# Order of the decay exponentials, half of bk on GpSimd, the last gates' tiles, and T4 ahead of T1 in a fox-attention + RWKV-7 block

## The chip, the cores and the metric

One core of one Trainium2 chip. The metric is the device time of one execution in microseconds (us). Engines: PE = TensorE (matrix products), DVE = VectorE, ACT = ScalarE, POOL = GpSimd, SP = the queue that issues most of the DMAs. Each engine takes its instructions in the order in which they stand in its queue; one engine meets another only where an instruction waits for a semaphore.

## The reference

One residual block over 1024 tokens of width 1024, float32:

```python
u = modulate(rms_norm(h), shift1, scale1)
proj = u @ w_in                               # fox q,k,v,f | rwkv r,k,v,w,a,g | two gates
o_fox  = fox_attention(q, k, v, log_f)        # 8 heads of 64, causal, forget-gate bias
o_rwkv = rwkv7_time_mix(p_rwkv, ...)          # 8 heads of 64, state 64x64
merged = sigmoid(gate_fox) * (o_fox @ fox_w_out) + sigmoid(gate_rwkv) * (o_rwkv @ rwkv_w_out)
h = h + gate1 * (merged @ w_o)
u2 = modulate(rms_norm(h), shift2, scale2)
a, b = split(u2 @ w_up); a = causal_conv3(a) + conv_b
h = h + gate2 * ((silu(a) * b) @ w_down)
return rms_norm(h, final_g)
```

The RWKV-7 mix runs, for each token, `state = state * w + (state a) b^T + v k^T` and `y = state r`, with `w = exp(-exp(w_log))`; the kernel does it in chunks of 64 tokens, and the products of decays inside a chunk are exponentials of a running sum, exp(-DEC*cum) and exp(+DEC*cum).

## The kernel before

**Stages.** Normalisation and low-rank inputs (0 to about 120 us of the profiled span), the fox and RWKV projections and the first RWKV preparation (to 240), the RWKV units with projections and, from about 450, the output gates between their matmuls (240 to 615), attention by heads with the remaining gates between (615 to 830), the two branch products and `w_o` (to 1005), the up projection of the feed-forward part in 22 column blocks (1005 to 1430), and the down projection (to 1647). Large products are done in three passes: both operands are split into a high and a low part (`u_hi`, `u_lo`; `hi_in`, `lo_in`), and high x high, low x high and high x low are added in PSUM.

**Who sets the order.** PE's order is written out by a small planner, `Weave`, which runs generators of matmuls against each other by estimated times, so it is fixed when the program is made. In the RWKV stage the order of DVE, ACT, SP and POOL is set by the tile framework's scheduler, from the order of the code, data and buffer dependencies, and its own timing; the kernel can add a dependency between two instructions (`tc.add_manual_dep`), which the scheduler then keeps as an order. In attention and from the up projection on, the order on DVE and ACT (there on SP too) is that of the code.

**The RWKV units.** There are eight units, k = 0..7: four pairs of heads (p) by two halves of the sequence (hf) of 512 tokens, eight chunks of 64 each. Three things go on at once. The main chain of unit k: `sp` matmuls (L141) add the old state into the chunk's sum, ACT scales the result into the next state S (L903), one chunk after another (the second half of a pair needs seven states, the first eight); then `yp`, the copy `y` (L915) and the group norm. Two units ahead, `pre` makes the operands of unit k+2: `ar` (L737, L741), `bk` (L739, L744), of which a copy of one half is repeated (L740), then the pair products `p` and `E` (L764), a triangular solve in steps of DVE (`t`, L784, and `E`, L786) on masks `M` that come by `sm` (L772) and `M` (L776) over SP. Three units ahead, the decay: `cum` is loaded by SP (L711) from DRAM, scanned by DVE (L715), and `el`, `en` are made from it by ACT (L719, L721). `cum`, `el`, `en` and `bk` have one buffer each: a new `el` waits for the reader of the old one (`ar`, L741), a new `en` for the old one's (`bk`, L744), a new load of `cum` for the old one's (`en`, L721).

**The gates.** `gate_steps` makes one gate in two halves: a product `gt` in PSUM, then on ACT Abs (L337), Exp (L338), Ln (L339), on DVE a difference (L340), on ACT the last Exp (L341), and SP writes the result `gs` to DRAM (`d_gate`, L342). The tile `gs` comes from a pool (`gsp`, tag `sp0`). At the passage to attention the heads' operands (`stA`, `stB`, `vh`) are loaded by POOL's queue. The gates made during attention have one PSUM tile, `rk_ps`, which two ACT instructions (L1162, L1163) read before the next product may write it. The softmax of the first key blocks uses a tile with the tag `Ps` of the pool `at`, two buffers.

**The up projection.** A column block takes seven products, k = 1..7 (a 2x2 scheme of Strassen's kind), each of one sum of quarters of the weights and one sum of quarters of the input: k=4 uses the input sum T4 (tiles `T_h`), k=5 the sum T1 (tiles `T_m`, `T_e`), k=3 B22 (`B_e`, `B_m`). PE takes them in the order of `plan` (L1606, L1607), entries (block, k), and their operands are made some products ahead on ACT and DVE. Results (`X`, `Y`, `W`) are taken from PSUM by ACT copies (L1559, L1568).

Of the kernel before, what the change touches and what calls it, by code (L numbers as in the profile page):

```python
# [9 lines left out]
F32 = mybir.dt.float32  # L10
F32R = mybir.dt.float32r
AF = mybir.ActivationFunctionType
# [4 lines left out]
S = 1024  # L17
KT = 8
NH = 512
# [7 lines left out]
DEC = math.exp(-0.5)  # L27
# [8 lines left out]
NOSYNC = mybir.DependencyInfo(mybir.DependencyClass.NoSync, mybir.DependencyReason.DATA)  # L36
# [96 lines left out]
def hybrid_block(ctx: ExitStack, tc: tile.TileContext, a, out):  # L133
    nc = tc.nc
# [107 lines left out]
            nc.vector.tensor_tensor(dst[:, cs], ps, bb[:, cs], op=ALU.add)  # L242

    marks = {}
    late_lo = deque()

    def lower(wait=0):
# [79 lines left out]
    def gate_steps(w, i, pps, ptag, pool, tag):  # L327
        if weave.late == 1:
            yield from late_gate(w, i)
            return  # L330
        for hf in range(2):
            cs = slice(hf * NH, hf * NH + NH)
            ps = pps.tile([128, NH], F32, tag=ptag, name=f"gt{i}_{hf}")
            yield from gemm_steps(ps, w, u, cs)

            g = pool.tile([128, NH], F32, tag=tag, name=f"gs{i}_{hf}")
            nc.scalar.activation(g, ps, AF.Abs)  # L337
            nc.scalar.activation(g, g, AF.Exp, scale=-1.0)  # L338
            nc.scalar.activation(g, g, AF.Ln, bias=1.0)  # L339
            stt(g, ps, 0.0, g, op0=ALU.min, op1=ALU.subtract)  # L340
            nc.scalar.activation(g, g, AF.Exp)  # L341
            nc.sync.dma_start(d_gate[i, :, cs], g)  # L342


# [1 line left out]
    with ExitStack() as es:  # L346
# [7 lines left out]
        def gen(name):  # L354
            return pr.tile([128, NH], F32, tag="gen", name=name)
# [202 lines left out]
        with tc.tile_pool(name="lg", bufs=1, reuse_waits="tile") as lg, \  # L558
# [47 lines left out]
            last = []  # L606
# [68 lines left out]
        def c3(ap):  # L675
            return ap.rearrange("p (c s) -> p c s", s=CH)
# [21 lines left out]
        def pre(k, p, hf):  # L698
# [5 lines left out]
            def tmp(nm, w=NH, bufs=1, dt=F32):  # L704
                return rw.tile([128, w], dt, tag=nm, name=f"{nm}{n}", bufs=bufs)

            def chunk_tile(nm, bufs, *dims):
                return rw.tile([128, *dims], F32, tag=nm, name=f"{nm}{n}", bufs=bufs)

            cum = tmp("cum")  # L710
# [5 lines left out]
                                             op0=ALU.mult, op1=ALU.add)  # L716
            el = chunk_tile("el", 1, NCU, CH + 1)
            nc.gpsimd.memset(el[:, :, 0:1], 1.0)
            nc.scalar.activation(el[:, :, 1:], c3(cum), AF.Exp, scale=-DEC)  # L719
            en = tmp("en")  # L720
            nc.scalar.activation(en, cum, AF.Exp, scale=DEC)  # L721
            ksq = tmp("ksq")
            nc.scalar.activation(ksq, kk, AF.Square, scale=V("k_k", p))
            parts = rw.tile([128, 3, NH], F32R, tag="bk", name=f"kp{n}")
# [8 lines left out]
            bk = chunk_tile("bk", 1, NCU, 3, CH)  # L733
# [3 lines left out]
            stt(ar[:, 0], c3(kr), nkk[:, p : p + 1], el[:, :, 0:CH], op0=ALU.mult, op1=ALU.mult)  # L737
            stt(kr, kr, V("k_k", p), al, op0=ALU.mult, op1=ALU.mult)
            tt(bk[:, :, 0, :], c3(kr), c3(en), op=ALU.mult)  # L739
            nc.scalar.copy(bk[64:128, :, 2, :], bk[64:128, :, 0, :])  # L740
            tt(ar[:, 1], c3(rr), el[:, :, 1:], op=ALU.mult)  # L741
            ts(al, al, V("k_a", p), oka[:, p : p + 1], op0=ALU.mult, op1=ALU.add)
            tt(al, al, kk, op=ALU.mult)
# [1 line left out]
            pcd = chunk_tile("pcd", 3, NCU)  # L745
# [11 lines left out]
            for c0 in range(0, NCU, 4):  # L757
                ps = [gen(f"p1_{n}{h}{c0}") for h in range(2)]
# [42 lines left out]
            vt, at = gen(f"vt{n}"), gen(f"at{n}")  # L801
# [11 lines left out]
            ps = [gen(f"tb{n}{h}") for h in range(2)]  # L813
# [16 lines left out]
        def main(k, p, hf):  # L830
# [3 lines left out]
            pcd, ar, E, QA, TT, bon, UV = (o[k] for k in ("pcd", "ar", "E", "QA", "TT", "bon", "UV"))  # L834
# [6 lines left out]
            for h in range(2):  # L841
                i = nc.vector.transpose(X[B0[h], :, :], TT[B0[h], :, 0:32])
# [20 lines left out]
            for c0 in range(0, NCU, 4):  # L863
                ps = gen(f"uw{n}{c0}")
                for c in range(c0, c0 + 4):
                    for h in range(2):
                        x = (c - c0) * 128
# [7 lines left out]
            for c0 in range(0, NCU, 4):  # L875
                ps = gen(f"mz{n}{c0}")
                for c in range(c0, c0 + 4):
                    for h in range(2):
                        x = (c - c0) * 128
# [8 lines left out]
            sp = py.tile([128, NCU, CH], F32, tag="sp", name=f"sp{n}")  # L888
            S = [state.get(p)]
# [8 lines left out]
            last_c = NCU - 1 - hf  # L898
            for c in range(last_c + 1):
                if S[c] is not None:  # L900
                    mm(sp[:, c, :], Mt[:, c, :], S[c], start=False, stop=c == last_c, more=True)
                S.append(rw.tile([128, CH], F32, tag="state", name=f"S{n}{c}", bufs=8))
                marks["S"] = nc.scalar.activation(S[-1], sp[:, c, :], AF.Copy, scale=pcd[:, c : c + 1])  # L903
                if c + 1 < NCU:
                    yield 1150

# [79 lines left out]
    fxp = ctx.enter_context(tc.tile_pool(name="fxp", bufs=1, reuse_waits="tile"))  # L986
    es = ExitStack()
    at = es.enter_context(tc.tile_pool(name="at", bufs=2, reuse_waits="tile"))
    pl = es.enter_context(tc.tile_pool(name="pl", bufs=2, space=PS))
    pt = es.enter_context(tc.tile_pool(name="pt", bufs=2, space=PS))  # L990
    heads = {}
# [239 lines left out]
    if "rest" in marks:  # L1231
        g, m = (gsp.tile([128, NH], F32, tag="sp0", name=f"rest{k}") for k in range(2))
        i = nc.scalar.activation(g, marks["rest"], AF.Abs)
# [33 lines left out]
    last = {}  # L1267
# [55 lines left out]
    for x in range(2):  # L1323
        for n in range(8):
            if x or n:
                k = 8 * x + n + 1
# [277 lines left out]
        put(6, s1[:, NH:])  # L1604

    plan = [(i, k) for ks in ((1, 2), (7,), (6,)) for i in range(2) for k in ks]  # L1606
    plan += [(0, 4), (0, 5), (1, 5), (1, 4), (0, 3), (1, 3)] + [(2, k) for k in (1, 7, 6, 2, 4, 5)]  # L1607
    for i in range(3, NFF):
        plan += [(i, 1), (i, 7), (i - 1, 3)] + [(i, k) for k in ((6, 2, 4, 5) if i < NFF - 1 else (6, 2, 5, 4))]
    plan.append((NFF - 1, 3))  # L1610
# [36 lines left out]
    ps = {t: [bank(k, f"wo{t}_{c}") for c, k in enumerate(ks)] for t, ks in enumerate(((0, 5), (6, 7), (1, 2)))}  # L1647
# [19 lines left out]
    ps = wo_do(3, 3)  # L1667
# [7 lines left out]
    ps = wo_do(4, 0)  # L1675
# [15 lines left out]
    for t, k in ((5, 2), (6, 6), (7, 4)):  # L1691
        ps = wo_do(t, k)
# [234 lines left out]
    for s, k in enumerate(ORDER):  # L1927
        ps = banks[4:] if k in (7, 4, 2) else banks[0:4]
# [109 lines left out]
```

## Time and profile before

| | |
|---|---|
| three runs | 1647.03, 1654.52, 1655.5 us; median 1654.52 |
| the profiled execution | 1648.91 us, span 1647.1 us |
| mean granted clock of PE | 0.995 |
| instructions | 25947 |
| DMA, HBM read and written | 173.35 and 65.54 MB |

The times of the runs are whole executions; the profile is one execution, and its span runs from the first to the last instruction. A row of a wait says which instruction was waited for, on which engine and at which line; the time is the engine's idle time. In a row of instructions the start comes first, then the time, and in brackets the idle time just before and what ended it. The name of a tile stands without its number; `gs<-gt` reads "gs is written from gt".

### The profile page before, as it was taken

How to read it: one execution, taken by the hardware profiler on the slowest of the kernel's cores; microseconds unless marked ns; L12 is line 12 of the kernel's file. 1: busy time of each engine (PE TensorE's matmuls, PEld its weight loads, DVE VectorE, ACT ScalarE, POOL GpSimd, SP SyncE). 2: the span in 40 equal slices, each digit the busy share in tenths (PEclk: the TensorE clock that was granted, in tenths of full speed). 3: DMA queues.
4: the chain of work that ended last, by engine and by line, in shares of the span. 5: the costliest groups of instructions: out<-in, count | busy, mean ns of one | idle time of the engine just before them, and what ended most of it. 6: DMA issues, size and time to landing. Idle time of an engine off the chain costs nothing.

```text
span 1647.1 us, 25947 instructions
## 1 busy us (share of the span) xinstructions
PE 1607.8 (98%) x9694; PEld 1339.6 (81%) x9694; DVE 1222.6 (74%) x2373; ACT 820.9 (50%) x1537; POOL 130.8 (8%) x153
## 2 busy tenths in 40 slices
PE   7999999999999999999999999999999999999998
PEld 7777788798978788888888888788888888888886
DVE  5786787878876526888679447887777777886677
ACT  5563335445445646766623235644444444555455
POOL 0011101111111010221022000000000000000000
PEclk9999999999999999999999999999999999999999
DMA  8488645543332346433197420242232232675363
GB/s 339 138 326 242 178 123 143 134 123 94 107 115 85 97 126 157 129 117 106 56 353 270 168 81 26 84 134 97 96 119 98 96 109 96 225 254 160 122 211 109
DMA packets 121645, 240.59 MB, mean 146 GB/s; under 512 B 40048, under 2 KB 48880, under 8 KB 121520
## 3 DMA queue, kind: packets, MB, share of 16 engines
q1 hardware_dynamic: 113040, 220.58, 41.0%
q0 software_dynamic: 8480, 18.37, 4.2%
q8 instruction: 76, 1.25, 0.3%
q14 instruction: 49, 0.40, 0.1%
HBM read 173.35 MB, written 65.54 MB: 145 GB/s over the span
## 4 chain that ended last, share of the span: by engine, by line
PE 58%; DVE 5%; ACT 2%; DMA 2%; issue 1%; SPq 0%; ACTq 0%; DVEq 0%
PE X L141 13%; PE D L141 13%; PE Y L141 6%; PE wo L141 5%; PE br L141 4%; PE rk_ps L141 3%; PE W L141 3%; PE gt L141 3%; PE lg L141 2%; PE ov L141 2%; PE tp L145 2%; DMA d_gate<-gs 1%; DVE nm L1049 1%; DVE P L1059 1%; DVE tl L1089 0%
## 5 line engine op out<-in xcount | busy, mean ns | idle before, releaser
L141 PE MATMUL D<-op,op 128*128 128x512 f32 x924 | 209.8, 389 | 0.0
L141 PEld LDWEIGHTS D<-op,op 128*128 128x128 f32 x924 | 173.3, 188 | 36.3 <-DVE op L1261 0.3
L141 PE MATMUL X<-T_m,S 128*128 128x512 f32 x440 | 107.8, 390 | 1.6 <-ACT T_m L1722 1.1
L141 PEld LDWEIGHTS X<-T_m,S 128*128 128x128 f32 x440 | 82.4, 188 | 20.4 <-ACT T_m L1722 2.5
L1260 ACT CAST op<-g 128x512 fp32r<-128x512 f32 x77 | 47.8, 621 | 73.8 <-PE D L141 49.0
L1261 DVE TENSOR_TENSOR op<-g,op 128x512 fp32r<-128x512 f32 x77 | 53.0, 688 | 41.4 <-ACT op L1260 41.4
L1519 DVE SCALAR_TENSOR_TENSOR c<-ab,vec,c 128x512 f32<-128x512 f32 x88 | 65.9, 750 | 18.4 <-ACT c L1522 16.8
L784 DVE TENSOR_TENSOR t<-E,M 128x60 f32<-128x60 f32 (+24 forms) x248 | 55.6, 224 | 27.9 <-DMA M<-sm 21.8
L1485 DVE TENSOR_TENSOR A<-ur,A 128x512 fp32r<-128x512 f32 x64 | 44.0, 688 | 38.7 <-ACT A L1481 38.5
L1485 DVE TENSOR_TENSOR S<-ur,S 128x512 fp32r<-128x512 f32 x66 | 45.5, 691 | 35.2 <-ACT S L1481 35.1
L274 DVE TENSOR_TENSOR lo_in<-raw_in,hi_in 128x512 fp32r<-128x512 f32 x84 | 56.7, 712 | 17.6 <-PE gt L141 4.8
L1481 ACT CAST S<-ur 128x512 fp32r<-128x512 f32 x66 | 41.0, 622 | 55.8 <-DVE ur L1474 30.6
L141 PE MATMUL Y<-T_h,S 128*128 128x512 f32 x264 | 63.6, 390 | 0.4 <-ACT T_h L1740 0.4
L141 PE MATMUL Y<-T_h,A 128*128 128x512 f32 x264 | 63.7, 389 | 0.3 <-ACT T_h L1722 0.3
L1053 ACT ACTIVATE P<-lg,nm 128x896 f32<-128x896 f32 (+3 forms) x64 | 47.4, 743 | 30.7 <-DVE nm L1049 22.5
L1481 ACT CAST A<-ur 128x512 fp32r<-128x512 f32 x64 | 39.6, 622 | 43.1 <-PE X L141 31.3
L786 DVE TENSOR_TENSOR E<-E,t 128x60 f32<-128x60 f32 (+24 forms) x248 | 56.2, 227 | 6.4
L141 PE MATMUL W<-B_f,A 128*128 128x512 f32 x252 | 60.6, 389 | 0.0
L141 PE MATMUL X<-B_b,A 128*128 128x512 f32 x252 | 60.5, 389 | 0.0
L141 PEld LDWEIGHTS Y<-T_h,S 128*128 128x128 f32 x264 | 49.5, 188 | 11.1 <-ACT T_h L1740 0.8
L141 PEld LDWEIGHTS Y<-T_h,A 128*128 128x128 f32 x264 | 49.5, 188 | 10.9 <-ACT T_h L1722 0.7
L272 ACT CAST hi_in<-raw_in 128x1024 fp32r<-128x1024 f32 x42 | 43.8, 1048 | 26.3 <-PE ps_rkv L141 11.3
(483 smaller groups left out, 4134.4 us busy)
## 6 DMA issues: line engine op xcount, KB each, us to landing
raw_in<-in_w_in SPq DMA_DIRECT2D x50, 512.0 KB, 4.0
wm<-in_w_mod SPq DMA_DIRECT2D x48, 512.0 KB, 7.3
ur<-in_w_up SPq DMA_DIRECT2D x44, 512.0 KB, 3.8
g<-d_g SPq DMA_DIRECT2D x35, 512.0 KB, 4.0
d_g<-gs SPq DMA_DIRECT2D x44, 256.0 KB, 2.0
d_g<-c SPq DMA_DIRECT2D x33, 256.0 KB, 4.4
d_st<-qh SPq DMA_DIRECT2D x64, 128.0 KB, 2.5
stA<-d_st POOLq DMA_DIRECT2D x8, 1024.0 KB, 6.9
```

What stands on the lines that cost most here:

```text
L141: nc.tensor.matmul(o, lhsT, rhs, start=start, stop=stop, skip_group_check=more)
L145: nc.tensor.transpose(o, i, eye)
L272: nc.scalar.copy(hi, raw)
L274: nc.vector.tensor_tensor(lo[:, c : c + NH], raw[:, c : c + NH], f32(hi[:, c : c + NH]), op=ALU.subtract)
L784: tt(tv, E32[:, 0:J, s : s + 1].to_broadcast([128, J, W]), M32[:, s : s + 1, s + 1 : 32].to_broadcast([128, J, W]), op=ALU.mult)
L786: tt(E32[:, 0:J, s + 1 : 32], E32[:, 0:J, s + 1 : 32], tv, op=ALU.add)
L1053: nc.scalar.activation(e[:, 0:n], lg[:, 0:n], AF.Exp, bias=nm[:, 0:1], accum_out=nm[:, 1:2])
L1260: nc.scalar.copy(hi, src)
L1261: tt(lo, src, f32(hi), op=ALU.subtract)
L1481: nc.scalar.copy(hi, src)
L1485: tt(lo, src, f32(hi), op=ALU.subtract)
L1519: stt(c, ab[:, x + hf * NH : x + hf * NH + NH], V("conv_w", 22 * x + i), c, op0=ALU.mult, op1=ALU.add)
```

## The change

Four edits. (1) The two exponentials `el`, `en` of a unit, which the scheduler was free to place anywhere, and the last exponential of each gate, get a dependency on the running chain of states. While a chain runs, they are held, and when its state is made, they are tied to it: the gates' exponential to the next state, `el` and `en` to the last state of the chain; outside a chain they are tied to the state made last. (2) The copy of half of `bk` goes from ACT to GpSimd. (3) From the moment that the attention pool `at` exists, a gate's `gs` is a tile of its tag `Ps`, no longer `sp0`, and the first ACT instruction of a gate follows the last one of the gate before. (4) In the list of products of the first two column blocks, (1, 4) comes ahead of (0, 5) and (1, 5).

```diff
+    held = {False: [], True: []}
+
+    def behind_state(i, next_one=False):
+        if marks.get("chain"):
+            held[next_one].append(i)
+        elif "S" in marks:
+            tc.add_manual_dep(i.ins, marks["S"].ins.name, NOSYNC)
+
+    def state_done(i, last):
+        marks["S"], marks["chain"] = i, not last
+        for x in held[True] + (held[False] if last else []):
+            tc.add_manual_dep(x.ins, i.ins.name, NOSYNC)
+        held[True].clear()
+        if last:
+            held[False].clear()
...
-            g = pool.tile([128, NH], F32, tag=tag, name=f"gs{i}_{hf}")
-            nc.scalar.activation(g, ps, AF.Abs)
+            g = marks["spare"].tile([128, NH], F32, tag="Ps", name=f"gs{i}_{hf}", bufs=2) if "spare" in marks else \
+                pool.tile([128, NH], F32, tag=tag, name=f"gs{i}_{hf}")
+            i0 = nc.scalar.activation(g, ps, AF.Abs)
+            if "spare" in marks and "gate_end" in marks:
+                tc.add_manual_dep(i0.ins, marks["gate_end"].ins.name, NOSYNC)
...
-            nc.scalar.activation(g, g, AF.Exp)
+            marks["gate_end"] = nc.scalar.activation(g, g, AF.Exp)
+            behind_state(marks["gate_end"], True)
...
-            nc.scalar.activation(el[:, :, 1:], c3(cum), AF.Exp, scale=-DEC)
+            behind_state(nc.scalar.activation(el[:, :, 1:], c3(cum), AF.Exp, scale=-DEC))
             en = tmp("en")
-            nc.scalar.activation(en, cum, AF.Exp, scale=DEC)
+            behind_state(nc.scalar.activation(en, cum, AF.Exp, scale=DEC))
...
-            nc.scalar.copy(bk[64:128, :, 2, :], bk[64:128, :, 0, :])
+            nc.gpsimd.tensor_copy(bk[64:128, :, 2, :], bk[64:128, :, 0, :])
...
-                marks["S"] = nc.scalar.activation(S[-1], sp[:, c, :], AF.Copy, scale=pcd[:, c : c + 1])
+                state_done(nc.scalar.activation(S[-1], sp[:, c, :], AF.Copy, scale=pcd[:, c : c + 1]), c == last_c)
...
+    marks["spare"] = at
...
-    plan += [(0, 4), (0, 5), (1, 5), (1, 4), (0, 3), (1, 3)] + [(2, k) for k in (1, 7, 6, 2, 4, 5)]
+    plan += [(0, 4), (1, 4), (0, 5), (1, 5), (0, 3), (1, 3)] + [(2, k) for k in (1, 7, 6, 2, 4, 5)]
```

The changed kernel's line numbers are higher by 16 to 21 than those of the kernel before (L903 is now L923, L715 is L735). The order of the instructions changes at more places than the diff shows, since the scheduler places the rest anew. Three of them, on engines whose queues the steps below go through:

ACT in the state chain of unit k=1. `S_10` to `S_16` are its states; `el_0_3408` and `en_0_3411` belong to unit k=4, `bk_1_2864` to k=3; `hi_in` is an operand of a projection, `qh` a result of one. Before:

```order
L719 ACTIVATE el_0_3408<-cum_0_3402 128x8x64
L740 COPY bk_1_2864<-bk_1_2864 64x8x64
L272 COPY hi_in_3026<-raw_in_3024 128x1024
L721 ACTIVATE en_0_3411<-cum_0_3402 128x512
L903 ACTIVATE S_10_3010<-sp_1_2947,pcd_1_1759 128x64
L393 ACTIVATE qh_1_3014<-qk_1_2914 128x512
L692 COPY kr_1_3340<-ksq_1_2991 128x512
L903 ACTIVATE S_11_3038<-sp_1_2947,pcd_1_1759 128x64
```

and now:

```order
L288 COPY hi_in_3026<-raw_in_3024 128x1024
L923 ACTIVATE S_10_3010<-sp_1_2947,pcd_1_1759 128x64
L413 ACTIVATE qh_1_3014<-qk_1_2914 128x512
...
L743 ACTIVATE ksq_0_3413<-k_2763,vec 128x512
L923 ACTIVATE S_16_3108<-sp_1_2947,pcd_1_1759 128x64
L739 ACTIVATE el_0_3408<-cum_0_3402 128x8x64
L741 ACTIVATE en_0_3411<-cum_0_3402 128x512
L935 COPY y_1_3132<-yp_1_2946 128x512
```

`el` and `en` moved from ahead of the first state to behind the last one, and the copy of `bk` has left this queue.

DVE at the place in which the scan of `cum_1_4281`, of unit k=5, now stands, between the two pairs of E products of k=3 (`E_1_3090`); `t_0_2563` and `E_0_2561` are steps of the solve of k=2, `sh_rkv` and `k` belong to a projection. Before, the scan stood amid the solve:

```order
L786 TENSOR_TENSOR E_0_2561<-E_0_2561,t_0_2563 128x7x5
L715 TENSOR_SCALAR cum_1_4281<-cst_120,cum_1_4281 128x256 x2
L784 TENSOR_TENSOR t_0_2563<-E_0_2561,M_0_2556 128x28
...
L764 TENSOR_TENSOR E_1_3090<-p_1_100_3093,cst_120 128x4x128
L764 TENSOR_TENSOR E_1_3090<-p_1_110_3094,cst_120 128x4x128
L764 TENSOR_TENSOR E_1_3090<-p_1_104_3135,cst_120 128x4x128
```

and now:

```order
L784 TENSOR_TENSOR E_1_3090<-p_1_100_3093,cst_120 128x4x128
L784 TENSOR_TENSOR E_1_3090<-p_1_110_3094,cst_120 128x4x128
L735 TENSOR_SCALAR cum_1_4281<-cst_120,cum_1_4281 128x256 x2
L784 TENSOR_TENSOR E_1_3090<-p_1_104_3135,cst_120 128x4x128
L784 TENSOR_TENSOR E_1_3090<-p_1_114_3136,cst_120 128x4x128
L862 STREAM_TRANSPOSE X_0_3376<-TT_0_2631 32x256 x2
L831 COPY QA_1_3091<-at_1_3250 64x4x64 x4
```

The scan moved back by some dozen instructions and across one pair of E products. The scans of k=4 and k=6 moved in the same way, to just ahead of the QA copies and of a pair of `lo_in`; that of k=7 stayed.

SP around the load of the same `cum_1_4281` (`se`, `TT`: the solve's results on their way; `raw_v`: weights; `sm`: masks of k=3). Before:

```order
L711 DMA cum_1_4281<-d_lora 128x512
L399 DMA d_st<-qh_1_3014 64x512 x4
L399 DMA d_st<-ql_1_3016 64x512 x2
L260 DMA raw_v_3278<-in_w_v 128x1024
L789 DMA se_0_2626<-E_0_2561 256x1x32 x4
L260 DMA raw_v_3285<-in_w_v 128x1024
L797 DMA TT_0_2631<-se_0_2626 32x8x32 x4
L772 DMA sm_1_3162<-E_1_3090 32x8x32 x4
```

and now:

```order
L809 DMA se_0_2626<-E_0_2561 256x1x32 x4
L276 DMA raw_v_3278<-in_w_v 128x1024
L817 DMA TT_0_2631<-se_0_2626 32x8x32 x4
L276 DMA raw_v_3285<-in_w_v 128x1024
L731 DMA cum_1_4281<-d_lora 128x512
L792 DMA sm_1_3162<-E_1_3090 32x8x32 x4
L796 DMA M_1_3167<-sm_1_3162 32x1024 x4
```

The load went from ahead of the six `d_st` writes to just ahead of `sm`.

## The prediction

> **What bounds the kernel now.** I read the page's busy times first, then the chain that ended last, then the waits of TensorE (PE) in order of size. The first two rows are the page's; in the others the columns are the idle total, how often, and the longest, in us.
>
> ```profile
> PE 1607.8 (98%) x9694; PEld 1339.6 (81%) x9694; DVE 1222.6 (74%) x2373; ACT 820.9 (50%) x1537; POOL 130.8 (8%) x153
> PE 58%; DVE 5%; ACT 2%; DMA 2%; issue 1%; SPq 0%; ACTq 0%; DVEq 0%
> ...
> PE rk_ps L141 <- ACT gm L1163: 3.1, 3, 1.9
> PE sp L141 <- ACT S L903: 2.8, 4, 1.4
> PE qk L141 <- DVE ql L395: 2.3, 1, 2.3
> PE ov L141 <- DVE o L1122: 2.0, 1, 2.0
> ...
> PE X L141 <- ACT T_m L1722: 1.1, 2, 0.9
> ...
> PE X L141 <- ACT x L1559: 0.5, 1, 0.5
> ...
> PE v L141 <- DVE v L369: 0.3, 1, 0.3
> ```
>
> PE is busy 1607.8 of 1647.1 us. The change removes no PE work, so it can win only from the 39.3 us in which PE stands, and from the time at half clock that follows some of those stalls. The waits it touches are `rk_ps` (3.1), `sp` (2.8) and `X` on `T_m` (1.1): 7.0 us, 0.4% of the span, at the very most, plus clock. The large stalls at the start (in the first 190 us) are not touched. So what decides is whether the new order brings stalls of its own; PE has no idle time to absorb them.
>
> **1. The decay exponentials behind the state chain.** The RWKV part runs eight units k=0..7; while the chain of states of unit k runs (matmul `sp`, then the ACT copy S, L903), the operands of unit k+2 and the exponentials `el`, `en` of unit k+3 are made. ACT takes its instructions in order. This is ACT in the chain of k=1, then what PE saw:
>
> ```profile
> 292.98 0.63 ACT L719 ACTIVATE el<-cum 128x512 f32<-128x512 f32 x1 [6.15 <-DVE ar L741]
> 294.56 0.62 ACT L740 COPY bk<-bk 64x512 f32<-64x512 f32 x1 [0.95 <-DVE bk L739]
> 295.21 1.05 ACT L272 CAST hi_in<-raw_in 128x1024 fp32r<-128x1024 f32 x1
> 296.47 0.63 ACT L721 ACTIVATE en<-cum 128x512 f32<-128x512 f32 x1 [0.21 <-DVE bk L744]
> 297.01 0.29 ACT L903 ACTIVATE S<-sp,pcd 128x64 f32<-128x64 f32 x1
> ...
> 297.36 0.43 PE L141 MATMUL sp<-S,Mt 128*128 128x64 f32 x2 [1.38 <-ACT S L903]
> ...
> 538.95 0.43 PE L141 MATMUL sp<-S,Mt 128*128 128x64 f32 x2 [0.83 <-ACT S L903]
> ```
>
> `el` may not overwrite its buffer before `ar` (L741) of the unit before has read it, and `en` not before `bk` (L744); the state copy S stood behind both and PE stood 1.38 us. With `el`, `en` and the `bk` copy out of the way S follows its `sp` at once. Of the four waits (2.8 us), the one at 538.95 (0.83) stands where no `el` or `en` is left to make, since that unit has none after it; it stays. The rest, 2.8 - 0.8 = 2.0 us, go: about 0.3 in the chain of k=0, 1.4 in k=1, 0.3 in k=4. Bounds: 0 (another ACT instruction takes their place) and -2.0. I take -2.0, since no instruction with a wait on DVE is left between the copies there.
>
> The two exponentials (0.63 us each) now run after the last S. In k=1..7 their reader, the next unit's `ar`, is several us away; at worst they push the copy of `y` by 1.26 us. No loss.
>
> **2. Half of bk on GpSimd.** The 0.62 us ACT copy, eight times, becomes one of GpSimd. The nearest row there is a cast of four times the elements:
>
> ```profile
> L266 POOL CAST hi_in<-raw_in 128x1024 fp32r<-128x1024 f32 x6 | 6.2, 1038 | 25.4 <-PE rk_ps L141 15.3 <-issue 5.4 <-PE gt L141 4.7
> ```
>
> So 0.5 to 1.0 us, on an engine that is 8% busy. Readers of that half, the `p` matmuls, also need the half that DVE writes about 2 us later (L744). Cost zero; without that cover up to 0.4 us a unit, 3.2 us in all, which I hold for the range only.
>
> **3. What the exponentials take with them: the scan of cum.** `cum` has one buffer. Its load (L711, on SP) for unit k+1 may overwrite it only when `en` of unit k has read it, and the DVE scan (L715) waits for the load. `en` late means load and scan late. The order listing shows the scans of k=4, 5 and 6 in new places, in DVE's in-order queue ahead of work that PE needs. Rows: the scan, the load's issue and its landing; ACT's last state copy of k=2's chain; SP and DVE around the new place in k=5, and PE where it ends:
>
> ```profile
> L715 DVE TENSOR_TENSOR_SCAN cum<-cst,cum x16: 659/672/706, 148.2 to 407.6; 128x256 f32<-128x256 f32 x16
> L711 SPq DMA_DIRECT2D cum<-d_lora x8: 325/335/550, 144.7 to 403.9; - x8
> DMA to landing us min/median/max: 2.5/2.9/3.7
> ...
> 306.19 0.31 ACT L903 ACTIVATE S<-sp,pcd 128x64 f32<-128x64 f32 x1 [0.18 <-PE sp L141]
> ...
> 307.15 1.82 SPq L797 DMA_DIRECT2D TT<-se  x4
> 313.51 1.71 SPq L776 DMA_DIRECT2D M<-sm  x4
> ...
> 309.80 1.29 DVE L764 TENSOR_TENSOR E<-p,cst 128x512 f32<-128x512 f32 x2 [3.15 <-PE p L141]
> 317.78 0.18 DVE L784 TENSOR_TENSOR t<-E,M 128x31 f32<-128x31 f32 x1
> 325.99 0.74 DVE L369 SCALAR_TENSOR_TENSOR v<-ps_rkv,omu,sh_rkv 128x512 f32<-128x512 f32 x1
> ...
> 326.79 0.85 PE L141 MATMUL v<-hi_v,u_hi 128*128 128x256 f32 x5 [0.29 <-DVE v L369]
> ```
>
> k=5: `en` of k=4 now ends at 306.50 + 2 x 0.63 = 307.8, up to 1.7 earlier if the gain of part 1 holds. SP reaches the load behind the four TT (end 308.97; they come some 1.3 earlier because two scans have left the 32x32 solve ahead of them, 2 x 0.67) and a `raw_v`: issue at 308.1 to 308.4. With 2.9 us to land (2.5 to 3.7) that is 310.6 to 312.1; the scan's 1.34 us ends at 312.0 to 313.4. On DVE it now stands ahead of the second pair of E products, which began at 309.80: 2.2 to 3.6 us later. From E the way goes by two SP loads (`sm`, M) to the solve whose first step stood at 317.78; M's issues ended at 315.22 and land some 2 us on, so 0.6 us of the delay is taken up: the solve starts 1.6 to 3.0 late, and `v` (L369), which stands in it by order, with it. PE had no slack at 326.79; it waited already. So PE, which would have been 1.7 us ahead here, is instead about 2.4 us behind the old time: it loses what part 1 gave and 2.4 us more. Bounds: +1.6 and +3.0; if the listing's place did not delay anything, -1.7.
>
> ```profile
> 264.64 1.73 DVE L811 COPY QA<-at 64x256 f32<-64x256 f32 x4 [1.54 <-PE at L145]
> ...
> 359.76 2.50 DVE L274 TENSOR_TENSOR lo_in<-raw_in,hi_in 128x512 fp32r<-128x512 f32 x4
> 362.51 1.72 DVE L811 COPY QA<-at 64x256 f32<-64x256 f32 x4
> ...
> 364.38 1.15 PE L141 MATMUL q<-UV,E 64*64 64x64 f32 x32
> ```
>
> k=4: the scan stands ahead of the QA copies, where DVE idled 1.54 us; the load may take 0.3 to 1.7 more, and what is lost here lies before the reset in k=5, so it adds nothing to the sum. k=6: the scan stands ahead of `lo_in` and QA, and DVE had no idle time there. The load waits for `en` of k=5, at about 357, and for SP; landed at about 360.2, scanned at 361.5: 1.8 us later than `lo_in` began. `q` on PE started 0.15 us after QA, but 0.5 to 1.3 us of other matmuls can stand ahead; I take +0.9 (0.5 to 1.4). k=7's scan keeps its place. After this only the 0.3 us of k=4's chain is won.
>
> **4. The last gates' tiles.** ACT and PE at the passage to attention, and the clock in three stretches (columns: PE, weight loads, DVE, ACT, GpSimd busy, then the granted clock, DMA share, GB/s):
>
> ```profile
> 618.05 0.60 ACT L337 ACTIVATE gs<-gt 128x512 f32<-128x512 f32 x1 [4.64 <-DMA d_gate<-gs]
> 621.74 0.59 ACT L1163 ACTIVATE gm<-rk_ps 128x512 f32<-128x512 f32 x1
> ...
> 622.39 2.05 PE L141 MATMUL rk_ps<-u_hi,hi_in 128*128 128x512 f32 x5 [1.93 <-ACT gm L1163]
> ...
> 190.00:192.00 2.00, 2.00 (x6) 1.56 (x5) 1.73 (x9) 0.00 (x0) 0.00 (x0) 0.50 0.86 158
> ...
> 624.00:626.00 2.00, 2.00 (x7) 1.54 (x6) 1.44 (x3) 0.63 (x1) 0.00 (x0) 0.50 1.17 194
> ...
> 674.00:676.00 2.00, 0.12 (x1) 0.12 (x2) 1.94 (x4) 2.00 (x6) 0.00 (x0) 1.00 0.87 143
> ```
>
> ACT waited 4.64 us for the gate before to be written out, because its buffer was the same. With other buffers it starts by 617.2 at the latest and is done (3.2 us of work from 618.05 to 621.27) before PE's product is ready at 622.39 - 1.93 = 620.46. The two reads of `rk_ps` then take 621.27 to 622.33, 1.06 us, from 620.46 on: the gap falls from 1.93 to about 1.1, -0.8. The half clock that follows this gap lasts about 3.4 us and costs half of it, 1.7, if it goes. A clock drop followed the gaps of 2.3 (at 187) and 1.93 us here, none followed the gap of 2.0 at 674, and none a gap of 1.4; at 1.1 it should stay full. But PE, 2.5 us early, runs on to logits whose operands come by DMA at the same moment as before, so I keep two thirds: -1.7 (bounds -0.8 and -2.5).
>
> [...]
>
> **5. T4 ahead of T1.**
>
> ```profile
> 1033.36 1.02 PE L141 MATMUL X<-T_m,S 128*128 128x512 f32 x2 [0.90 <-ACT T_m L1722]
> ...
> 1054.26 2.12 PE L141 MATMUL X<-T_m,S 128*128 128x512 f32 x8 [0.52 <-ACT x L1559]
> ```
>
> Doing both T4 products first gives `T_m` 2.7 us (twelve matmuls) more, so the 0.9 us and its tail, 2.1 us in all, go. But at 1054.26 PE waits for an ACT copy behind the same DVE work as before, so it would wait there for what it saved. Net 0 (bounds -2.1 if that copy moves too, +1.0 if the last sums, now made in another order, are late).
>
> **Sum**, on the profiled execution (1648.91 us, span 1647.1 and 1.8 around it): after k=5 +2.4, k=6 +0.9, k=4's chain -0.3, gates -1.7, T4 0: +1.3, 1650.2 us. The runs shown lie at 1647.03, 1654.52 and 1655.5, so the profiled one is 0.3% under the median; by the median the same sum gives 1655.8. A new median can fall at either level; I predict 1654.5.
>
> **Rivals.**
> (a) Slower: the late scan of `cum` decides. The stalls at E, `q` and `v` merge into one of over 2 us in k=5 and again in k=6, each followed by a half clock like that at 624 (1.7): 3.0 + 1.7 + 1.4 + 1.7 - 0.3 - 0.8 + 1.0 = +7.7, 1656.6 on the profiled execution, 1662 by the median. It decides from a load landing after 312. For it: DVE has no idle to give at 359.76. Against: the delays fall on three places, each under 2 us.
> (b) Faster: the loads land in time, parts 1, 4 and 5 keep all: -2.0 - 2.5 - 2.1 = -6.6, 1642.3, 1648 by the median. For it: each wait is real on PE. Against: the scan's row and landing above.
> (c) It does not do what it says: the state copies wait for PE and the other ACT work instead, scans included, and all is hidden or absorbed: 0, 1648.9 or 1654.5. For it: the ACT waits named are mostly off PE's path. Against: 1.38 us at 297.36.
> [...]
>
> **How the numbers follow.** Forecast 0.40, (a) 0.22, (b) 0.18, (c) 0.15, (d) 0.05. The forecast's own range is -0.9 to +3.0 around the sum. The range goes down to 1645 (half of (b) on the lower level of the runs) and up to 1663 ((a) by the median). 0.5%, 8.3 us, is about what a measurement tells from no change; no sum reaches it alone. Slower: four fifths of (a), whose 7.7 lies just under, when the runs' spread or a third half clock (1.7) comes on top, 0.18. Faster: over half of (b) with the same help, 0.11, and 0.03 of the rest. Within: 0.68.
>
> **What would show it.** Right: no `sp` wait on S before 500; DVE idle before `cum` L715 (now L735) ended by its load, near 310 and 360; TensorE waits on `v`, `q` or `mu` near 313 to 328; full clock after 620 with a gap near 1.1; no wait on `T_m`, a longer one on `x`. Wrong: if scans do not wait, (b); if PE's idle in 240 to 450 grows by over 6 us, (a).

## The result, and the profile after

The changed kernel takes 1662.49 us (median of six runs, 1660.63 to 1664.1). Beside it the kernel before was run three times more: its six runs have a median of 1649.11 us (1647.03 to 1655.5). The ratio is 1.0077, 95% interval 1.006 to 1.0094: slower by 0.77%, about 12.7 us. Both profiled executions lie close to their medians, 1648.91 and 1662.75 us, 13.8 us apart.

TensorE's waits in the kernel after, in order of size (total, times, longest, in us):

```profile
PE idle L141 <- DMA cst<-in_cst: 6.8, 1, 6.8
PE mps L141 <- DVE acc L474: 3.4, 1, 3.4
PE mu L141 <- DVE E L784: 3.2, 1, 3.2
PE qk L141 <- DVE ql L415: 2.6, 1, 2.6
PE q L141 <- DVE QA L831: 2.6, 3, 2.1
PE sp L141 <- ACT S L923: 2.6, 3, 1.2
PE rk_ps L141 <- ACT gm L1184: 2.3, 3, 1.2
PE v L141 <- DVE vs L975: 2.0, 3, 1.0
PE ov L141 <- DVE o L1143: 2.0, 1, 2.0
...
PE X L141 <- DVE Ze_a L1587: 1.4, 2, 1.2
```

Two waits at the places that the late scan was to reach are new and large, on E (3.2) and on QA (2.1). The wait on the state copies, which the first edit was to take away, has hardly changed: 2.6 us after 2.8. `rk_ps` fell from 3.1 to 2.3; the wait on `T_m` is gone and one on `Ze_a`, an operand sum of the up projection, has come.

TensorE does its matmuls in nearly the same order in both kernels, so the same matmul can be looked up in both traces. The table gives the start of some in the one and the other; what the difference grows by from row to row is what was lost between them.

| place | before, us | after, us | behind by |
|---|---|---|---|
| a `ps_rkv` product at the end of the first preparation | 209.4 | 210.7 | +1.4 |
| a `ps_rkv` product in k=1's chain | 300.0 | 302.6 | +2.6 |
| `mu` of k=1, after the E products of k=3 | 313.46 | 319.42 | +6.0 |
| `v` products | 340.3 | 349.5 | +9.2 |
| `q` of k=4 | 364.38 | 375.89 | +11.5 |
| `ps_rkv` products, half clock over | 380.8 | 393.9 | +13.1 |
| end of the RWKV chains | 612.4 | 627.3 | +15.0 |
| gates in attention, after the first | 632.4 | 645.0 | +12.6 |
| first `X` on B_e of the up projection | 1042.70 | 1056.44 | +13.7 |
| last matmul | 1639.2 | 1652.6 | +13.4 |

The first 1.4 us can't be laid to the change: a run below with the plan alone, in which all engines keep the order of the kernel before up to the up projection, is 3.4 us ahead at the same place. Of the 13.4 us, 10.4 are lost between 300 and 381. This is the scan of k=5 in ACT, SP, DVE and TensorE of the kernel after:

```profile
309.55 0.62 ACT L741 ACTIVATE en<-cum 128x512 f32<-128x512 f32 x1
...
310.32 1.82 SPq L817 DMA_DIRECT2D TT<-se  x4
312.24 0.40 SPq L276 DMA_DIRECT2D raw_v<-in_w_v  x1
312.68 0.43 SPq L731 DMA_DIRECT2D cum<-d_lora  x1
...
307.98 1.29 DVE L784 TENSOR_TENSOR E<-p,cst 128x512 f32<-128x512 f32 x2
317.41 1.28 DVE L735 TENSOR_TENSOR_SCAN cum<-cst,cum 128x256 f32<-128x256 f32 x2 [8.14 <-DMA cum<-d_lora]
318.60 1.26 DVE L784 TENSOR_TENSOR E<-p,cst 128x512 f32<-128x512 f32 x2
...
327.71 0.19 DVE L804 TENSOR_TENSOR t<-E,M 128x31 f32<-128x31 f32 x1 [2.57 <-DMA M<-sm]
...
319.42 0.47 PE L141 MATMUL mu<-Ztr,blk_r 128*128 128x512 f32 x1 [3.17 <-DVE E L784]
...
333.12 1.10 PE L141 MATMUL v<-lo_v,u_hi 128*128 128x256 f32 x4 [1.21 <-DVE lo_v L290]
```

The exponential `en` ended at 310.2. SP came to the load only at 312.68, behind four TT and a `raw_v`; the scan, which needs the load landed, began 4.7 us after that. DVE stood 8.14 us before the scan, with the second pair of E products behind it and their inputs there since 312.4. TensorE reached `mu` and stood 3.17 us: in the code `mu` takes its PSUM tile from the same four buffers (tag `gen`) as the products `p`, and the row names E, the reader of `p`. The solve, which waits for E by way of `sm` and M, began only at 327.71, and `lo_v`, which stands amid it on DVE, held `v` for another 1.21 us. In k=6 the scan stands ahead of `lo_in` and QA in the same way:

```profile
370.11 1.28 DVE L735 TENSOR_TENSOR_SCAN cum<-cst,cum 128x256 f32<-128x256 f32 x2 [0.83 <-ACT hi_in L288]
371.30 2.47 DVE L290 TENSOR_TENSOR lo_in<-raw_in,hi_in 128x512 fp32r<-128x512 f32 x4
374.03 1.71 DVE L831 COPY QA<-at 64x256 f32<-64x256 f32 x4
...
375.89 1.77 PE L141 MATMUL q<-UV,E 64*64 64x64 f32 x32 [2.09 <-DVE QA L831]
```

(The row of the scan names the cast `hi_in`, which the scan doesn't read; in the run with the exponentials alone the same scan waits 0.98 us, and there the row names its load.) Both losses are followed by a stretch at half clock, from 335.21 and from 376.17. The windows by time (columns as in the prediction; granted clock third from the end):

```profile
336.00:338.00 2.00, 2.00 (x23) 1.94 (x20) 1.97 (x6) 0.73 (x2) 0.00 (x0) 0.50 0.62 216
...
376.00:378.00 2.00, 2.00 (x33) 1.88 (x33) 1.45 (x6) 1.25 (x2) 0.09 (x1) 0.54 0.96 289
...
636.00:638.00 2.00, 1.40 (x6) 1.18 (x7) 0.23 (x1) 1.70 (x4) 0.00 (x0) 1.00 1.37 207
```

At 636, where the gates pass to attention, the clock now stays full, as the prediction had it; what that is worth, the experiments show.

### The profile page after: what moved, and what is told of

Its sections match the earlier page's. It is cut to its first block, busy times and chain, and to the rows that moved or that the text cites. A ratio compares the mean times of both kernels' runs of the same rounds, so it can differ in the third digit from the quotient of the medians.

```text
span 1660.5 us, 25964 instructions
## 1 busy us (share of the span) xinstructions
PE 1610.7 (97%) x9694; PEld 1341.2 (81%) x9694; DVE 1228.2 (74%) x2373; ACT 815.9 (49%) x1529; POOL 136.7 (8%) x161
## 4 chain that ended last, share of the span: by engine, by line
PE 59%; DVE 5%; ACT 2%; DMA 1%; issue 1%; SPq 0%; ACTq 0%; DVEq 0%
PE X L141 13%; PE D L141 13%; PE Y L141 7%; PE wo L141 5%; PE br L141 4%; PE gt L141 4%; PE rk_ps L141 3%; PE W L141 3%; PE lg L141 2%; PE ov L141 2%; PE tp L145 2%; DVE P L1080 1%; DVE nm L1070 1%; DVE tl L1110 0%; DMA d_gate<-rest 0%
## 5 line engine op out<-in xcount | busy, mean ns | idle before, releaser
L804 DVE TENSOR_TENSOR t<-E,M 128x60 f32<-128x60 f32 (+24 forms) x248 | 59.8, 241 | 27.8 <-DMA M<-sm 21.7
```

The lines of the kernel that those rows point to most:

```text
L804: tt(tv, E32[:, 0:J, s : s + 1].to_broadcast([128, J, W]), M32[:, s : s + 1, s + 1 : 32].to_broadcast([128, J, W]), op=ALU.mult)
```

## The experiments

Theory A: the loss comes from `el` and `en` tied to the end of the chain, through `cum`'s single buffer: its load is late, and the scan stands in DVE's queue ahead of work that TensorE waits for. Rival B: the `bk` copy on GpSimd hinders DVE and costs most of it. The ratios are to runs of the kernel before made beside each group, with the 95% interval.

**The exponentials free again** (the changed kernel without their tie):

```diff
-            behind_state(nc.scalar.activation(el[:, :, 1:], c3(cum), AF.Exp, scale=-DEC))
+            nc.scalar.activation(el[:, :, 1:], c3(cum), AF.Exp, scale=-DEC)
-            behind_state(nc.scalar.activation(en, cum, AF.Exp, scale=DEC))
+            nc.scalar.activation(en, cum, AF.Exp, scale=DEC)
```

> The changed kernel with el and en not tied to the state chain (everything else of the change kept). Theory A (the late load and scan of cum hold DVE): the scans stand again in their old places, so TensorE has no stall over 1 us at mu, q or v between 300 and 380 and no half clock there; of the change stay the gates' gain (2.4 us) and the plan's loss (0.8): 1646 to 1650 us. Rival B (the bk copy on GpSimd slows DVE, 5 us or more): 1654 us or above, stalls near 320 and 370 stay.

Measured: 1652.36 us, ratio 1.0020 (1.0009 to 1.0031). The waits at `mu` and `q` near 316 and 373 are gone, and so is the half clock there: 0.57 of the 0.77% lost come back. But the time is 2.4 us above the range given for theory A: something in the rest of the change costs as well.

**The exponentials alone** (the kernel before with `held`, `behind_state` and `state_done` for `el` and `en` only).

> The kernel before with el and en tied to the end of the state chain and nothing else. Theory A: the whole loss of the RWKV stage is here, without the gates' gain of 2.4 us: 1659 to 1665 us, mu waits about 3 us near 316 and q about 2 us near 373, with half clock behind. Rival B: no copy on GpSimd, so most of the loss is gone: 1655 us or less.

Measured: 1659.03 us, ratio 1.0057 (1.0036 to 1.0078). TensorE's waits in it:

```profile
PE mu L141 <- DVE E L783: 3.4, 1, 3.4
PE q L141 <- DVE QA L830: 3.0, 2, 2.2
PE sp L141 <- ACT S L922: 2.4, 3, 1.1
PE rk_ps L141 <- ACT gm L1182: 2.3, 3, 1.2
```

Both stalls are there without the other three edits: the tie by itself costs about 9.4 us (0.57%). And `rk_ps` stands at 2.3 as in the kernel after, although the gates' tiles are those of the kernel before. More on that below.

**The scan behind the QA copies**, all else as in the change:

```diff
+                scan = nc.vector.tensor_tensor_scan(cum[:, c0 : c0 + 256], ...)
+                if k in (4, 5, 6):
+                    tc.add_manual_dep(scan.ins, marks[f"QA{k - 2}"].ins.name, NOSYNC)
```

> The changed kernel with one more order: the scans of cum of k=4, 5 and 6 stand behind the QA copies of k=2, 3 and 4 on DVE, so that a scan that waits for its load holds up neither E products nor QA. el and en stay tied. Theory A: the stalls at mu (3.2), v (1.2) and q (2.1) and the two half clocks (1.7 each), 9.9 us in all, go or shrink to under 2: 1651 to 1655 us. Rival B: the scan's place is not it: 1659 us or more.

Measured: 1655.41 us, ratio 1.0023 (1.0009 to 1.0038). This DVE stretch of it stands at the place of the stall:

```profile
308.49 1.29 DVE L786 TENSOR_TENSOR E<-p,cst 128x512 f32<-128x512 f32 x2
312.93 1.29 DVE L786 TENSOR_TENSOR E<-p,cst 128x512 f32<-128x512 f32 x2 [3.15 <-PE p L141]
...
316.56 1.73 DVE L833 COPY QA<-at 64x256 f32<-64x256 f32 x4 [1.52 <-PE at L145]
318.31 1.29 DVE L290 TENSOR_TENSOR lo_v<-raw_v,hi_v 128x512 fp32r<-128x512 f32 x2
319.52 1.27 DVE L735 TENSOR_TENSOR_SCAN cum<-cst,cum 128x256 f32<-128x256 f32 x2
```

The E products wait for their matmuls again, 3.15 us as before the change, and the scan finds its load landed. One order on DVE, with the exponentials still tied and their load still late, takes back 0.54 of the 0.77%: it is the scan's place in the queue, together with the late load, that costs. The median is 0.4 us above the range given; the rest is looked for in the copy and the plan.

**The load earlier, the scan's place kept** (`el` and `en` tied to the fourth state of the chain instead of the last):

```diff
+                if c == 3:
+                    marks["early"] = marks["S"]
...
+        if not next_one:
+            if "early" in marks:
+                tc.add_manual_dep(i.ins, marks["early"].ins.name, NOSYNC)
```

> The changed kernel with el and en behind the fourth state of the running chain, no longer behind the last. The scan of k=5 keeps its new place on DVE between the pairs of E products; only its load can come some 4 to 5 us earlier. Theory A in the form 'the landing of the load decides, not the place of the scan': the stall at mu falls from 3.2 us to under 1 and that at q in k=6 to under 1, 1650.5 to 1656 us. Rival (the place of the scan alone costs it): mu 2 us or more, 1658 us or above.

Measured: 1657.36 us in four runs, ratio 1.0055 (1.0036 to 1.0074): by the time between the two, above theory A's range and below the rival's. The waits moved as theory A has it: the scan of k=5 still stands between the E products, waits less than half as long, and `mu` starts without a wait; `q` in k=6 waits 1.1 us instead of 2.1.

```profile
311.52 0.88 SPq L734 DMA_DIRECT2D cum<-d_lora  x1
...
316.94 2.20 DVE L738 TENSOR_TENSOR_SCAN cum<-cst,cum 128x256 f32<-128x256 f32 x2 [3.62 <-DMA cum<-d_lora]
...
320.11 0.39 PE L141 MATMUL mu<-Ztr,blk_r 128*128 128x512 f32 x1
```

From 310 to 381 TensorE loses 2.4 us in it (behind by 6.7, then by 9.1), where the kernel after loses 10.4: with the scan in the same place, the landing decides. Counted without what TensorE was behind by, the load is issued 5.2 us earlier (311.52 - 6.7 against 312.68 - 2.6). Of these 8.0 us the total shows 5.0 (the last matmul is 8.4 us behind, after 13.4), because this version loses more ahead of the place: 5.1 us by 300, against 2.6, and then 1.9 us at a state copy up to 304, with a half clock behind it. Of the 5.1 us, 2.7 stand there by 209, where profiles of the same order differ by as much; why it loses more after that was not tried.

**The copy on GpSimd alone** (the kernel before with L740 on GpSimd).

> The kernel before with the copy of half of bk on GpSimd and nothing else. Theory A: the copy is free for TensorE to within 1.5 us: 1648 to 1651 us. Rival B: DVE and GpSimd hinder each other, DVE's small steps beside the copy get longer and the unit's chain with them, 1654 us or more.

Measured: 1652.43 us, ratio 1.0019 (1.0009 to 1.0029), about 3 us: above theory A's bound, below rival B's. The copy, DVE beside it, and TensorE in k=0's stretch:

```profile
249.66 0.81 POOL L740 COPY bk<-bk 64x512 f32<-64x512 f32 x1 [2.56 <-DVE bk L739]
...
249.44 0.54 DVE L742 TENSOR_SCALAR al<-al,vec,oka 128x512 f32<-128x512 f32 x1
249.90 0.61 DVE L784 TENSOR_TENSOR t<-E,M 128x24 f32<-128x24 f32 x1
250.54 0.75 DVE L369 SCALAR_TENSOR_TENSOR k<-ps_rkv,omu,sh_rkv 128x512 f32<-128x512 f32 x1
...
251.35 0.73 PE L141 MATMUL ps_rkv<-u_hi,hi_in 128*128 128x512 f32 x2 [1.43 <-DVE k L369]
```

A solve step `t` of 24 elements, 0.17 us in the kernel before, takes 0.61 us and ends when the copy ends; behind it `k` is late, for which TensorE waits. Only a part of the 1.43 us is the copy's: with the gates alone and with the plan alone, whose order here is that of the kernel before, the same row waits 0.56 us. In this run PE, DVE and SP keep the order of the kernel before throughout, and only the eight copies go from ACT's queue to GpSimd's, so no other order is behind its loss. In the kernel after, seven of the eight copies meet a two-input step of DVE, which takes 0.3 to 0.4 us longer each time. But the loss doesn't come in eight equal parts: from 205 to 275 us TensorE stands 4.2 us here and 1.8 us in each of those two runs, and that difference of 2.4 us is most of the 3; three of the eight copies have run by then. The step `al`, which reads one full tensor, takes 0.54 us beside the copy, as it does in the kernel before. Why the steps with two inputs take longer was not shown; these rows give only what it costs.

**The copy on DVE** (the kernel before with L740 on DVE), to tell DVE's time from GpSimd's longer way.

> The kernel before with the copy of half of bk on DVE, no GpSimd in it. Theory D (the copy on GpSimd costs through DVE's time: about 0.4 us for each of eight copies, in stretches in which TensorE waits for DVE): a copy of about 0.4 to 0.6 us in DVE's own queue costs about the same, 1650.5 to 1654 us. Rival L (it is GpSimd's longer way, 0.8 us from issue to the p products, that costs): within 0.7 us of before.

Measured: 1653.66 us, ratio 1.0033 (1.0018 to 1.0047); the copy takes 0.42 us. Rival L is out: with no GpSimd in it, the copy costs at least as much. This speaks for theory D but does not prove it, since here the scheduler also moved some dozens of DVE's instructions, and some of ACT's and SP's, and the new order may cost a part.

**The gates alone** (the kernel before with `Ps` tiles and `gate_end`).

> The kernel before with the gates' tiles of the passage from the attention pool (and the first ACT step of such a gate behind the last one of the gate before), nothing else. Theory G1 (ACT's wait for the gate's write was what held TensorE at 622): the gap there falls from 1.9 to about 1.2 us and the time by 0.7 to 2.4 us: 1646 to 1648.5 us. Theory G2 (the gap fell to 1.2 in two runs without this edit, since the write lands in time as soon as TensorE comes later; and the half clock only moves from 622 to 675): within 0.7 us of before.

Measured: 1648.40 us, ratio 1.0000 (0.999 to 1.001). In its profile, ACT does not wait for a write and TensorE waits 1.18 us, as predicted. But TensorE waits 1.18 us too in three kernels without this edit (the exponentials, the copy and the plan alone). The plan alone has the order of the kernel before up to here, so the 1.93 us there were one execution's luck. In the kernel with the copy on DVE, which has the old gate tiles, the wait was far longer:

```profile
628.15 0.60 ACT L337 ACTIVATE gs<-gt 128x512 f32<-128x512 f32 x1 [7.77 <-DMA d_gate<-gs]
...
632.48 1.03 PE L141 MATMUL rk_ps<-u_hi,hi_in 128*128 128x512 f32 x2 [5.06 <-ACT gm L1163]
```

In the eight profiles with the new tiles the gap is 1.17 or 1.18 us in all, and ACT never waits for a gate's write; in the five with the old ones ACT waits for it in four, 2.25 to 7.77 us, and TensorE's gap is 1.18 three times, 1.93 and 5.06. So the edit does away with ACT's wait, which reached TensorE only where it was longest (4.64 and 7.77). This looks like a tail that the median does not show; whether the long times become rarer with the edit, the twelve runs do not tell.

**The plan alone** (the kernel before with T4 ahead of T1).

> The kernel before with T4 ahead of T1 and nothing else. Theory P1 (three runs with the new plan lose 0.8 us there, two with the old none): the wait on T_m (0.9) goes, a wait on DVE's operands of B22 of about 1.2 us near 1042 takes its place, +0.8 us net: 1649 to 1651 us. Theory P2: no change or a gain of up to 2 us: 1646.5 to 1649 us.

Measured: 1649.79 us, ratio 1.0009 (0.9998 to 1.0021): not told from no change by the time. The profile shows the new wait, in the same place as in the kernel after:

```profile
1036.93 1.20 PE L141 MATMUL X<-T_m,S 128*128 128x512 f32 x4 [0.59 <-DVE S L1485]
1037.97 1.08 PE L141 MATMUL X<-T_e,S 128*128 128x512 f32 x4
1040.20 1.17 PE L141 MATMUL X<-B_e,S 128*128 128x512 f32 x4 [1.15 <-DVE Ze_a L1566]
```

TensorE falls back by 0.8 us net here in all five profiles with the new plan, which I take as its price; the runs allow anything from nothing to 3.5 us and don't show it.

**Repaired versions.** First the scan behind the QA copies, the copy on ACT and the old plan:

> The changed kernel with the scans of k=4, 5, 6 behind the QA copies, the bk copy back on ACT and the old order of T1 and T4: of the change only el and en behind the last state and the gates' tiles are left, without the scans' wait. Theory A plus the copy's and the plan's own costs (3 and 1 us): 1647 to 1650.5 us, within 0.15% of before. Rival (el and en behind the last state cost by themselves, through y, ar or pcd): 1652 us or more.

Measured: 1651.01 us, ratio 1.0010 (0.9998 to 1.0021), half a microsecond above the range given and below the rival's bound. Then the exponentials behind the second state, the copy on ACT and the old plan, the scans left to the scheduler:

> el and en behind the second state of the chain, the bk copy on ACT and the old order of T1 and T4, the gates' tiles as in the change. Theory A with the costs of the other parts: all losses gone, the wait of the state copy in k=1 (1.4 us) mostly won: 1645.5 to 1649 us, at or below the kernel before. Rival: any tie of el and en costs: 1651 us or more.

Measured: 1650.57 us, ratio 1.0008 (0.9998 to 1.0018), between theory A's range and the rival's: a wait of 0.7 us at `mu` and one of 0.5 at `v` are left of the scan's, and the state copy in k=1 waits 0.6 instead of 1.4. And both repairs together:

> The parts that cost nothing put together: el and en behind the second state of the chain (most of the state copy's wait in k=1 goes), the scans of k=4, 5, 6 behind the QA copies, the bk copy on ACT, the old order of T1 and T4, the gates' tiles as in the change. Theory A: no stall over 0.7 us from 240 to 400 and 1646 to 1649.5 us, at or a little under before. Rival (the ties of el and en cost by themselves, as the 0.1% of the two kernels like it may say): 1650 us or more.

Measured: 1647.88 us against 1649.65, ratio 0.9990 (0.998 to 1.000): the best of the versions, 1.8 us by the medians, and hardly to be told from the kernel before. The wait at the state copy of k=1 is down to 0.3 us, none is left on E, and the longest on QA or `v` is 0.3 us. The stalls over 0.7 us from 240 to 400 are not all gone: 0.72 us at 250 and 0.83 at 254 are left, at the rows that wait 0.56 and 0.83 us with the gates alone.

## Why the prediction was wrong

The time fell inside the range (1662.49, range to 1663) and the forecast was wrong: not within 0.5% but slower by 0.77%. On the scale of the profiled executions +13.8 us stand against a sum of +1.3. What happened is in kind rival (a), the late scan with two half clocks, but larger than its +7.7, and the price of the copy with it. The term that failed most is the place after k=5: +2.4 in the sum, +9.2 in the trace. By the table the 13.4 us at the last matmul are 2.6 by 300, 6.5 in k=5, 3.9 from there to 381, 1.9 to 612, -2.4 at the gates and +0.8 at the plan.

- **The state chain (predicted -2.0).** Not won. The step that failed was "no instruction with a wait on DVE is left between the copies". The cast `kr` stands between the first and the second state in k=1, and waits for a DVE step of the preparation:

```profile
300.70 0.62 ACT L712 CAST kr<-ksq 128x512 fp32r<-128x512 f32 x1 [2.21 <-DVE ksq L768]
301.23 0.31 ACT L923 ACTIVATE S<-sp,pcd 128x64 f32<-128x64 f32 x1
...
301.59 0.43 PE L141 MATMUL sp<-S,Mt 128*128 128x64 f32 x2 [1.20 <-ACT S L923]
```

The first state of k=1 no longer waited; the second did, 1.20 us. Of the three waits that were to go, that of k=0 rose from 0.30 to 0.53 us, that of k=1 fell from 1.38 to 1.20, and only the 0.25 us of k=4 went. The row of `kr` stood in the order listing; in the kernel before it passed without a wait, behind `en`. With the tie at the second state, the copy on ACT and the scans moved away (the last version) 1.1 of the 1.4 us were won.

- **k=5 (a swing from -1.7 to +2.4, that is 4.1 us).** The steps up to E were right: `en` late, the load late, the scan waiting ahead of the E products. The last step was not. I led the delay from E through `sm` and M to the solve and to `v`, and took PE to come out 2.4 us behind there; TensorE stood earlier and directly, 3.17 us at `mu`, whose PSUM buffer waits for E, and then 1.21 us more at `v` behind the solve. `mu` stands in my list of signs, but has no term in the sum. With the half clock the swing measured 6.5 us (from +2.6 at 300 to +9.2 at 340). The sizes: I had the load issued at 308.1 to 308.4; it was issued at 312.68, and 310.1 without the 2.6 us that TensorE was behind by then. The four TT ahead of it had not come 1.3 us earlier, as I took from the scans that left the solve: a solve step beside a GpSimd product (at 301.9) took 1.29 us instead of 0.19. The scan began 4.7 us after the issue, where I took 2.9 to the landing, the median of all (and 3.7 as the bound). The load now follows two 512 KB weight loads; that this is the reason was not tested. The half clock (1.7 us, from 335.2 on) I had put into the rival.

- **k=6 (predicted +0.9).** 3.5 us: `q` waited 2.09 us, above the bound of 1.4, and the half clock that I had not counted followed (1.7). k=4, which I had at nothing in the sum, was 0.3 us. Where k=4's chain was to give back 0.3, another 1.9 us were lost between 381 and 612, 1.6 of it in two waits of `v` on DVE's `vs`. That part I did not foresee. It goes with the tie to the last state, and neither with the copy nor with the scans of k=4 to 6: the four profiles with that tie lose 1.6 to 1.9 us there, among them the one with these scans moved and the copy on ACT (1.6); those with the tie loosened or left out lose 0.9 at most, the copy on DVE aside. In these four DVE stands 2.8 to 3.0 us ahead of the scan of k=7, which no version ties anew, against 1.6 in the kernel before; that this is the cause was not tested.

- **The copy on GpSimd (predicted 0, "up to 3.2 us, for the range only").** 0.19%, 3.1 us alone. I had looked for its price on ACT, GpSimd and the readers of `bk`; it was on DVE, which the profile of before had shown: a solve step at 318.17 took 1.23 us beside a GpSimd product, where the step at 317.78, ahead of that product, took 0.18. So the engines met here outside of the waits for semaphores too: the instruction itself took longer.

- **The gates (predicted -1.7).** The passage won 2.4 us in the two profiles compared, within the bounds; in the median it is nothing. The failing step was to price a wait by the one execution that showed it.

- **The plan (predicted 0).** The wait on the copy at 1053.74 did not take over the saving; a wait of 1.17 us on the operands of the next product did, as the upper bound (+1.0) had said: +0.8 in the trace.

- **The scale.** I took the profiled execution to be 0.3% under the typical one, from three runs. With six runs the median is where the profiled execution is.

What the single edits cost by their ratios, 0.57 + 0.19 + 0.00 + 0.09 = 0.85%, agrees with the 0.77% of all of them within the intervals. The tie of the gates' last exponential is in none of these four; the three repaired versions have it, and stand at 0.10, 0.08 and -0.10%.

## What to carry to other kernels

An instruction held back holds back what waits for its buffer: follow the single buffer upstream (here `en`, then `cum`'s load, then its scan) and look what stands behind the waiting instruction in each in-order queue, and which buffers the waiting work keeps from others (here the PSUM tile that `mu` needed); moving that one waiter behind the urgent work gave back more than two thirds of the loss (0.54 of 0.77%). A copy given to an idle GpSimd was paid for here by two-input work on DVE beside it (`t` took 0.61 us instead of 0.17), so price such a copy by DVE's time where TensorE waits for DVE. And a wait at a DMA's end that one profile shows may be a chance of that execution: look at it in several before counting its removal.

## What the runs showed of the hardware

Whether a stall was followed by a half clock went here with where it fell among windows of one length. Between 150 and 1600 us the granted clock of the kernel before is 0.50 from 189.45 to 192.87 us and from 622.95 to 626.36, that of the kernel after from 191.85 to 195.27, from 335.21 to 338.63 and from 376.17 to 379.59: 3.413 us each time. Within a profile the starts lie whole multiples of this length apart: 127.0 times in the kernel before, 42.0 and 12.0 times in the kernel after. Carried on from these starts, the multiples divide the whole profile into windows; that they hold also where the clock stayed full is an estimate from these numbers.

In all 13 profiles TensorE stands 1.95 to 1.98 us at the same `ov` matmul of attention; a window of 0.50 follows in six of them (the last version is one) and in the other seven none, the kernels before and after among them. It shifts TensorE by 1.5 to 1.6 us. In the six, 1.91 us or more of the gap lie within one such window; in the seven a border cuts it, and at most 1.74 us lie on one side. In the kernel before, for example, the gap runs from 673.91 to 675.88, and 622.95 + 15 x 3.413 puts a border at 674.15. The 3.17 us before `mu` in the kernel after, which brought no drop, are cut in the same way: from 376.17 back 17 windows is 318.15, which leaves 1.90 and 1.27 us.

From 150 to 1600 us, all 15 windows of the 13 profiles in which TensorE, at full clock, stood 1.91 us or more in all were followed by a half clock (2.31 and 1.93 us in the kernel before, 2.14 and 2.09 in the kernel after). Four half clocks came behind less, 1.90, 1.60 (ahead of 335.21 in the kernel after), 1.45 and 1.13 us, while other windows with up to 1.90 us (that ahead of 318.15 in the kernel after) were followed by none; what decides between them was not found. The one behind 1.13 us is in the run with the gates alone, where it began at 1034.6, with no gap above 0.90 us in the 15 us ahead of it:

```profile
1032.16 1.02 PE L141 MATMUL X<-T_m,S 128*128 128x512 f32 x2 [0.90 <-ACT T_m L1742]
1033.36 2.43 PE L141 MATMUL X<-T_m,S 128*128 128x512 f32 x6 [0.19 <-ACT T_m L1742]
...
1036.00:1038.00 2.00, 2.00 (x6) 1.59 (x5) 2.00 (x5) 0.95 (x2) 0.00 (x0) 0.50 0.04 8
```

So in these profiles the length of a gap did not decide by itself what followed it: the same 1.96 us at `ov` did both, as a border fell into it or not, and 3.17 us at `mu` brought no drop. My threshold in the prediction, a length of the gap between 1.4 and 1.9 us, does not hold as a length. What makes the clock drop, these traces do not show; the windows are only what went with it.
